# A hybrid decoder block: the down products in another order with four sums in one set of banks, gate operands one branch later, and four up weights in tiles of another pool

## The chip, the cores and the metric

The kernel runs on one core of a Trainium2 chip. The time is that of one execution on the device in microseconds; three timed runs of the kernel before gave 1117.07, 1119.05 and 1122.3 us, a median of 1119.05. One more execution was recorded by the hardware profiler: 1114.22 us, of which its span, from the first to the last recorded instruction, is 1112.4 us. Engines are called PE (the tensor engine; PEld is its weight load), DVE (vector), ACT (scalar), POOL (GpSimd) and SP, which here only issues transfers.

## The reference

One block on x of 1 x 1024 x 1024 in float32, with D_FF of 4096, cut to its core:

```
h = rmsnorm(x) @ w_in + b_in                 # 512 pool, 512 q, 128 k, 128 v, 2048 gates
y_pool = multiscale_pool(u) @ w_pool * pool_scale
y_attn = sliding window attention (window 128, 8 heads, 2 kv heads, sinks)
g_pool, g_attn = sigmoid(gates)
merged = g_pool * (y_pool @ w_branch_pool) + g_attn * (y_attn @ w_branch_attn)
x = x + rmsnorm(merged @ w_out)
ff = square(relu(rmsnorm(x) @ w_up)) @ w_down
return x + rmsnorm(ff)
```

## The kernel before

Every large product is made from pairs of reduced-precision operands: a value is split into a high half (a cast on ACT, line 101) and a low half (a subtraction on DVE, line 104), and PE runs three passes (high x high, low x high, high x low; PASSES). The largest products (gates, w_out, w_up, w_down) are cut into 2 x 2 blocks and computed with seven block products instead of eight, of which DVE forms sums and differences as operands and as results. So DVE and ACT prepare operands all the time and PE multiplies. Each engine works through its own queue in order; a scheduler of the tile framework sets those orders from the source and from priorities, so SP's order in particular is not that of the lines. Tiles come from pools of a fixed number of buffers; a load into a new tile waits for the last reader of the buffer's old tile.

Three places matter here.

**Gates (lines 913 to 1000).** The two branches are computed in eight steps m each. Step m makes one 128-row strip of a branch product in two "mm" banks (line 428), and DVE multiplies it into the gate tile z (line 933). Each step of even m loads two z tiles for two strips (line 922, "z loads", from the spilled gates). After each odd m, merge(m // 2) adds the pool branch's tiles to the attention branch's by two accumulating transfers on POOL (line 954, g<-g), for the last pair by DVE. From the merged tiles come the operands of the w_out products: gop[1] and gop[5] are made in steps m = 5 and 6 (lines 988 to 994) by split_pairs (high half, low half) and a subtraction (line 992). wo_weight loads the W_O weights of one product (line 970).

**Up products (lines 1200 to 1310).** The normalised x is transposed on PE (line 1081) from hs, which out_post makes for each of eight token tiles (lines 1039 to 1053): a load of x, mean square on ACT, reciprocal square root in small steps on DVE and ACT (lines 130 to 144), gain (line 1050), residual add (1051), store (1052). Pairs of w_up strips (UpPairs, 16 pairs; the first NF0 = 7 have their products 1 and 2 made early) are loaded (line 458) into a stage tile, and operand(p, i) splits them. prepare(p) is load(2p), operand(p, 1), operand(p, 2). The pool fp (12 tiles with tag "T") is opened here and is used for the third products' operands from build_second on.

**Down products (lines 1329 to 1476).** Seven products run in the order PRODUCTS, each over NS = 8 steps of two 128-row slices of D_FF, 192 matmuls a product, with operands made AHEAD = 2 steps before. Token tiles 0 to 3 (th = 0) and 4 to 7, and two column halves, make the four result blocks. A product sums over all its steps in four PSUM banks, "at" or "mm" in turn; 2 goes on top of 1 in the same banks, 3 on top of 5; the other sums are made by DVE from the copies u, v, c11, c12. The results get their square sums on ACT (fin_sq, line 1390), the gain on DVE (fin_gain, line 1393), rr by rsqrt_sum, and fin_out multiplies by rr, adds the x1 tile read from DRAM, and stores. The last product's last three steps (LATE) run token tile by token tile, so that each can be closed while PE works on the next.

Of the kernel before, what the change touches and what calls it, by code (L numbers as in the profile page):

```python
# [8 lines left out]
F32 = mybir.dt.float32  # L9
# [5 lines left out]
P = 128  # L15
# [3 lines left out]
NK = D // P  # L19
# [31 lines left out]
def block_kernel(ctx: ExitStack, tc, xt, x, consts, vecs, sinks, b_qkv, g_post, g_mlp_post,  # L51
# [20 lines left out]
    def stage(shape):  # L72
        return st.tile([P] + shape, F32, tag="st", name=nm("st"))
# [13 lines left out]
    def bank(tag, shape=None):  # L87
        return psum["pool"].tile([P] + (shape or [512]), F32, tag=tag, name=nm(tag), bufs=psum["bufs"][tag])
# [4 lines left out]
    def flat(t):  # L93
        return t.rearrange("p a b -> p (a b)")
# [879 lines left out]
    def merged(kh, th):  # L974
        return [zg[8, 2 * kh + j][th] for j in range(2)]

    def x_place(shape):
        return xp.tile([P] + shape, F32R, tag="x", name=nm("wo"))

    for m in range(8):  # L980
        branch(wbp_dram[m], lambda k, hl, th: ysp[k][hl][:, th * 512:(th + 1) * 512], 0, m)
        if m % 2:
            merge(m // 2)
        if m == 0:
            wo_weight(1, x_place)
        elif m == 2:
            wo_weight(5, x_place)
        elif m == 5:
            b11, b12 = merged(0, 1), merged(0, 0)
            gop[1] = split_pairs(b11, gr)  # L990
            for p_, q_ in zip(b11, b12):
                dve.tensor_tensor(p_, p_, q_, ALU.subtract)
        elif m == 6:
            gop[5] = split_pairs(b11, ar)
    xpool.__exit__(None, None, None)


# [234 lines left out]
        h, dj = B_OF[name]  # L1232
        return w_rows[s_, h][:, :, dj * 512:(dj + 1) * 512]

    up.prepare(3)
    up.prepare(4)
    up.load(0)
    up.load(1)
    def first_kt(kt):
# [8 lines left out]
    up.m2(0)  # L1248
    up.m2(1)
    up.m1(4, bank("mm"))  # L1250
    up.prepare(5)
    build_second(1)
    up.operand(0, 6)
    up.m1(5, bank("mm"))
    up.m2(2)
    up.prepare(6)
    build_second(2)
    build_third(0)
    up.operand(0, 7)
    up.m2(4)  # L1260
    up.m1(6, bank("mm"))
    b6, b7 = bank("at"), bank("at")
# [81 lines left out]
    def operands(i, s_):  # L1344

        if i == 1 and s_ in early_raw:
            ft, wt = early_raw[s_]
        else:
            ft = raw_tile()
            nc.sync.dma_start(ft, f_block(A_OF[i], s_))  # L1350
            if i == 1:
                resident("B11", s_)
                if s_ - 3 in early_raw:
                    resident("B11", s_ - 3)
                wt = res["B11", s_]
            elif i == 5:
                resident("B12", s_)
                wt = res["B11", s_]
                dve.tensor_tensor(wt, res["B12", s_], wt, ALU.subtract)  # L1359
            elif i == 2:  # L1360
                wt = streamed("B21", s_)
            elif i == 3:
                resident("B22", s_)
                wt = res["B22", s_]
            elif i == 6:
                wt = res["B11", s_]
                dve.tensor_tensor(wt, res["B22", s_], wt, ALU.subtract)
# [27 lines left out]
    def fin_half(n, dj, v):  # L1395
        fin_sq(n, dj, v)
        fin_gain(dj, v, v)
# [7 lines left out]
        dve.tensor_tensor(sq[:, dj, ns], sq[:, dj, ns], eps_y[:, ns], ALU.add)  # L1405

    def fin_out(n, hv):
        if n not in xf:
            t = stage([2, 512])
            nc.sync.dma_start(flat(t), x1_dram[n])  # L1410
            xf[n] = t
        for dj in (1, 0):
            o = xf[n][:, dj, :]
            dve.scalar_tensor_tensor(o, hv[dj][n % 4], rr[:, n:n + 1], o, ALU.mult, ALU.add)
            (nc.scalar if dj and n == NT - 1 else nc.sync).dma_start(out[n][:, dj * 512:(dj + 1) * 512], o)

    PRODUCTS = (1, 5, 2, 3, 6, 7, 4)
    LATE = 3
    steps = [(i, s_) for i in PRODUCTS for s_ in range(NS)]
    u, v, c11, c12 = acc4("u"), acc4("v"), acc4("c11"), acc4("c12")  # L1420
# [4 lines left out]
    for j, (i, s_) in enumerate(steps):  # L1425
        if j + AHEAD < len(steps):
            operands(*steps[j + AHEAD])
        if s_ == 0 and i not in (2, 3):
            tag = "mm" if i in (5, 7) else "at"
            banks[i] = [bank(tag) for _ in range(4)]  # L1430
        bs = banks[{2: 1, 3: 5}.get(i, i)]
        if i != 4 or s_ < NS - LATE:
            down_mm(i, s_, bs, i in (2, 3), [(s_, k2, t) for k2 in range(2) for t in range(4)])
            if s_ < NS - 1:
                continue
        elif s_ < NS - 1:
            continue
        for t in range(4):
            if i == 1:
                act.copy(u[t], bs[t])  # L1440
            elif i == 5:
                act.copy(v[t], bs[t])
            elif i == 2:
                act.copy(c11[t], bs[t])
                fin_half(t, 0, c11[t])
            elif i == 3:
                act.copy(c12[t], bs[t])
            elif i == 6:
                dve.tensor_tensor(u[t], u[t], bs[t], ALU.add)
                dve.tensor_tensor(c12[t], c12[t], u[t], ALU.add)  # L1450
                dve.tensor_tensor(v[t], v[t], u[t], ALU.add)
                fin_half(t, 1, c12[t])
            elif i == 7:
                dve.tensor_tensor(v[t], v[t], bs[t], ALU.add)
                dve.tensor_tensor(u[t], u[t], bs[t], ALU.add)
                fin_half(4 + t, 1, v[t])
            else:
                n = 4 + t
                down_mm(i, s_, bs, False, [(s2, k2, t) for s2 in range(NS - LATE, NS) for k2 in range(2)])
                dve.tensor_tensor(u[t], u[t], bs[t], ALU.add)  # L1460
                fin_sq(n, 0, u[t])
                fin_gain(0, c11[t], u[t])
                rsqrt_sum(rr[:, n:n + 1], sq[:, 0, n:n + 1], sq[:, 1, n:n + 1])
                fin_out(n, (c11, v))
        if i == 7:
            add_eps(slice(4, NT), 1)
            for n in range(4, NT):
                load_x1(n)
        if i == 6:
            add_eps(slice(0, 4), 1)  # L1470
            rsqrt_sum(rr[:, 0:4], sq[:, 0, 0:4], sq[:, 1, 0:4], 4)
            for n in range(4):
                fin_out(n, (c11, c12))
    rpool.__exit__(None, None, None)


# [70 lines left out]
```

## Time and profile before

| | before |
|---|---|
| timed runs | 1117.07, 1119.05, 1122.3 us; median 1119.05 |
| profiled execution | 1114.22 us |
| its span | 1112.4 us |
| mean granted clock | 1.00 in the windows shown below |
| DMA read, written | 152.99 MB, 63.96 MB |

A row of a timeline reads: start in us, length in us, engine, line, operation, out<-in, shape and count; in brackets how long the engine was idle just before and whom it waited for. A group row of a view by lines has the busy time of all, and the mean ns of one. SPq and POOLq rows are the issuing of transfers, not the transfers; "DMA" rows in the chain are the transfers. The names in out<-in are tile tags: g and gr, ar are gate tiles and operands, wh weight operands, st stage tiles, at and mm PSUM banks, sm small tiles of one column.

### The profile page before, as it was taken

The page shows a single profiled execution, that of the slowest core. Times are in us where ns is not written, and L with a number is a line of the kernel's source. Part 1 is how long each engine was busy: PE and PEld are TensorE (multiplying, and loading weights), DVE is VectorE, ACT ScalarE, POOL GpSimd, SP SyncE. Part 2 cuts the span into 40 slices and gives each one's busy share as a digit, 9 for nine tenths or more (in the row PEclk, how much of TensorE's full clock was granted, in tenths as well). Part 3 has the DMA queues.
Part 4 walks back from the last instruction along what each step waited for, and adds up shares of the span by engine and source line. Part 5 has one row for each costly group of instructions (what it writes and reads, how often), then busy time and mean ns, then how long its engine had stood idle before and what let it go on. Part 6 is the DMA issues. An engine that isn't in the chain of part 4 may idle for free.

```text
span 1112.4 us, 13921 instructions
## 1 busy us (share of the span) xinstructions
PE 1099.5 (99%) x5119; PEld 908.9 (82%) x5119; DVE 807.9 (73%) x1180; ACT 552.4 (50%) x921; POOL 59.8 (5%) x111
## 2 busy tenths in 40 slices
PE   9999999999999999999999999999999999999997
PEld 7888788888888878878888888888888888888885
DVE  5578867898868667989988767666548945447796
ACT  7466656444432326677555655444434435444342
POOL 0333221110000010000000000000000000000000
PEclk9999999999999999999999999999999999999999
DMA  9306569997676572563457645435697666332762
GB/s 349 140 11 136 149 147 344 232 318 248 216 250 221 152 186 74 195 232 109 145 202 259 243 174 195 155 143 209 216 363 247 231 192 196 104 96 73 223 191 81
DMA packets 91588, 212.63 MB, mean 191 GB/s; under 512 B 7616, under 2 KB 20032, under 8 KB 91456
## 3 DMA queue, kind: packets, MB, share of 16 engines
q1 hardware_dynamic: 78384, 180.54, 48.2%
q0 software_dynamic: 7520, 11.54, 6.3%
q10 hardware_dynamic: 5616, 19.66, 4.6%
q8 instruction: 40, 0.66, 0.2%
q14 instruction: 28, 0.23, 0.1%
HBM read 152.99 MB, written 63.96 MB: 195 GB/s over the span
## 4 chain that ended last, share of the span: by engine, by line
PE 82%; DVE 8%; DMA 5%; ACT 2%; issue 2%; DVEq 0%; POOL 0%; POOLq 0%; ACTq 0%; SPq 0%
PE mm L494 24%; PE at L494 16%; PE at L1384 15%; PE mm L1384 12%; PE mm L187 3%; PE mm L584 2%; PE at L1035 2%; DMA g<-g 1%; PE at L196 1%; PE mm L1035 1%; PE sc L187 1%; PE mm L428 1%; PE at L399 1%; DMA g<-spill_dram 1%; DVE gr L104 1%
## 5 line engine op out<-in xcount | busy, mean ns | idle before, releaser
L1384 PE MATMUL at<-ar,wh 128*128 128x512 f32 x744 | 169.6, 389 | 0.0
L1384 PEld LDWEIGHTS at<-ar,wh 128*128 128x128 f32 x744 | 139.6, 188 | 29.3 <-DVE ar L104 0.4
L1384 PE MATMUL mm<-ar,wh 128*128 128x512 f32 x576 | 131.0, 389 | 0.0
L104 DVE TENSOR_TENSOR wh<-raw,wh 128x1024 fp32r<-128x1024 f32 x53 | 64.8, 1223 | 89.7 <-ACT wh L101 89.7
L1384 PEld LDWEIGHTS mm<-ar,wh 128*128 128x128 f32 x576 | 108.1, 188 | 22.5
L101 ACT CAST wh<-raw 128x1024 fp32r<-128x1024 f32 x53 | 55.8, 1053 | 139.4 <-PE at L1384 62.4
L101 ACT CAST wh<-st 128x512 fp32r<-128x512 f32 (+1 forms) x107 | 68.4, 650 | 76.1 <-PE at L494 19.1
L104 DVE TENSOR_TENSOR wh<-st,wh 128x512 fp32r<-128x512 f32 (+1 forms) x107 | 76.8, 727 | 27.3 <-ACT wh L101 25.2
L494 PE MATMUL mm<-gr,wh 128*128 128x512 f32 x333 | 80.2, 391 | 0.0
L494 PEld LDWEIGHTS mm<-gr,wh 128*128 128x128 f32 x333 | 62.1, 188 | 12.8
L494 PE MATMUL mm<-T,wx 128*128 128x512 f32 x288 | 67.6, 389 | 0.0
L494 PEld LDWEIGHTS mm<-T,wx 128*128 128x128 f32 x288 | 54.1, 188 | 11.2
L494 PE MATMUL at<-T,wx 128*128 128x512 f32 x252 | 59.1, 389 | 0.0
L494 PEld LDWEIGHTS at<-T,wx 128*128 128x128 f32 x252 | 47.3, 188 | 9.8
L494 PE MATMUL mm<-x,wh 128*128 128x512 f32 x240 | 55.2, 389 | 0.0
L494 PEld LDWEIGHTS mm<-x,wh 128*128 128x128 f32 x240 | 45.0, 188 | 9.4
L584 PE MATMUL mm<-x,wh 128*128 128x512 f32 x192 | 47.8, 396 | 0.0
L104 DVE TENSOR_TENSOR ar<-B,ar 128x1024 fp32r<-128x1024 f32 x37 | 45.1, 1219 | 1.6 <-ACT ar L101 1.3
L584 PEld LDWEIGHTS mm<-x,wh 128*128 128x128 f32 x192 | 35.2, 188 | 7.7
L101 ACT CAST ar<-B 128x1024 fp32r<-128x1024 f32 x37 | 38.9, 1050 | 3.6 <-DVE B L1359 2.8
L494 PE MATMUL at<-gr,wh 128*128 128x512 f32 x150 | 36.6, 390 | 0.0
L101 ACT CAST wx<-ws 128x512 fp32r<-128x512 f32 x30 | 18.6, 620 | 33.9 <-DVE ws L470 19.1
(384 smaller groups left out, 2151.6 us busy)
## 6 DMA issues: line engine op xcount, KB each, us to landing
raw<-f_dram SPq DMA_DIRECT2D x53, 512.0 KB, 3.8
f_dram<-g SPq DMA_DIRECT2D x30, 512.0 KB, 3.3
st<-in_w_up_dram SPq DMA_DIRECT2D x24, 512.0 KB, 3.8
B<-in_w_dn_dram SPq DMA_DIRECT2D x24, 512.0 KB, 6.4
st<-in_w_g_dram SPq DMA_DIRECT2D x18, 512.0 KB, 6.9
f_dram<-g ACTq DMA_DIRECT2D x17, 512.0 KB, 3.0
g<-spill_dram SPq DMA_DIRECT2D x16, 512.0 KB, 6.3
raw<-in_w_dn_dram SPq DMA_DIRECT2D x16, 512.0 KB, 4.7
```

What stands on the lines that cost most here:

```text
L101: act.copy(hi, src)
L104: eng.tensor_tensor(lo, src, f32(hi), ALU.subtract)
L187: pe.matmul(bq, xs_[k][n // 4][:, xh, n % 4 * P:(n % 4 + 1) * P], wq[k][:, h, :], start=k == 0 and j == 0, stop=k == NK - 1 and j == 2)
L196: pe.matmul(bkv_of(n), xs_[k][n // 4][:, xh, n % 4 * P:(n % 4 + 1) * P], wkv[k // 2][:, h, k % 2, :], start=k == 0 and j == 0 and not (joi ...
L399: pe.matmul(flat(yb), v[:, kv, :], flat(p[:, 4 * kv:4 * kv + 4]), start=j == 0, stop=j == len(mms) - 1)
L428: pe.matmul(bs[th], whi[:, k, :], rhs(k, hl, th), start=k == 0 and hl == 0, stop=False)
L494: pe.matmul(b, w[:, wh, kt, :], xo[kt][:, xh, :], start=not after and kt == 0 and j == 0, stop=kt == 3 and j == 2, skip_group_check=after)
L584: pe.matmul(b, (whi, wlo)[h][:, k, :], xr(k, xh, th), start=j == 0, stop=j == len(mms) - 1)
L1035: pe.matmul(bs[t], gop[i][kt // 2][gh][:, kt % 2, t * P:(t + 1) * P], wop[i][kt // 2][wh][:, kt % 2], start=not after and kt == 0 and j == ...
L1384: pe.matmul(bs[t], fo[fh][:, k2, t * P:(t + 1) * P], wo_[wh][:, k2, :], start=not after and s2 == 0 and k2 == 0 and j == 0, stop=s2 == NS ...
```

## The change

It has three parts.

1. *Down order.* The order of products becomes 1, 5, 6, 3, 7, 2, 4. Products 1, 6, 7 and 4 sum in the same four "at" banks, 5 and 3 in "mm", and 2 in four "mm" banks of its own. The partial sums are read as they stand after a product: u after 1, v after 5, c12 after 6, v plus the bank after 7, and so on, so that twenty DVE additions go. The output of token tiles 0 to 3 is written in another way: x1 is copied to out from DRAM to DRAM by SP, ACT multiplies the results by rr in the steps s < 4 of product 4, and POOL adds them into out by accumulating transfers of 256 KB. For tiles 4 to 7 the square and the gain of the last product's results read its bank directly.
2. *Gate operands.* The operands gop[1] and the subtraction are made in m = 4 and 6 for one tile each, and gop[5] after the loop.
3. *Up weights.* The first strip of pairs 3 to 6 is loaded into a "T" tile of the pool fp (named wr), ahead of the first operands; prepare is gone there, and operand(0, 7) comes earlier.

```diff
+    b11, b12 = merged(0, 1), merged(0, 0)
     for m in range(8):
         branch(wbp_dram[m], lambda k, hl, th: ysp[k][hl][:, th * 512:(th + 1) * 512], 0, m)
...
-        elif m == 5:
-            b11, b12 = merged(0, 1), merged(0, 0)
-            gop[1] = split_pairs(b11, gr)
-            for p_, q_ in zip(b11, b12):
-                dve.tensor_tensor(p_, p_, q_, ALU.subtract)
-        elif m == 6:
-            gop[5] = split_pairs(b11, ar)
+        elif m in (4, 6):
+            j = m // 2 - 2
+            gop.setdefault(1, []).extend(split_pairs(b11[j:j + 1], gr))
+            dve.tensor_tensor(b11[j], b11[j], b12[j], ALU.subtract)
+    gop[5] = split_pairs(b11, ar)
...
-    up.prepare(3)
-    up.prepare(4)
+    for p in range(3, NF0):
+        up.load(2 * p, fp.tile([P, NK, P], F32, tag="T", name=nm("wr")))
+    for p in (3, 4):
+        for i in (1, 2):
+            up.operand(p, i)
...
             elif i == 3:
-                resident("B22", s_)
                 wt = res["B22", s_]
             elif i == 6:
+                resident("B22", s_)
                 wt = res["B11", s_]
...
-    PRODUCTS = (1, 5, 2, 3, 6, 7, 4)
+    PRODUCTS = (1, 5, 6, 3, 7, 2, 4)
...
-        if s_ == 0 and i not in (2, 3):
-            tag = "mm" if i in (5, 7) else "at"
-            banks[i] = [bank(tag) for _ in range(4)]
-        bs = banks[{2: 1, 3: 5}.get(i, i)]
+        if s_ == 0 and i in (1, 5, 2):
+            banks[i] = [bank("at" if i == 1 else "mm") for _ in range(4)]
+        bs = banks[{6: 1, 7: 1, 4: 1, 3: 5}.get(i, i)]
+        chained = i in (6, 7, 4, 3)
+        if i == 4 and s_ == 0:
+            add_eps(slice(0, 4), 1)
+            rsqrt_sum(rr[:, 0:4], sq[:, 0, 0:4], sq[:, 1, 0:4], 4)
+        if i == 4 and s_ < 4:
+            fin_gain(0, u[s_], u[s_])
+            for dj, t_ in ((1, c12[s_]), (0, u[s_])):
+                act.activation(t_, t_, AF.Identity, scale=rr[:, s_:s_ + 1])
+                pool.dma_start(out[s_][:, dj * 512:(dj + 1) * 512], t_, accum_op=ALU.add)
...
-            elif i == 2:
-                act.copy(c11[t], bs[t])
-                fin_half(t, 0, c11[t])
+            elif i == 6:
+                act.copy(c12[t], bs[t])
             elif i == 3:
-                act.copy(c12[t], bs[t])
-            elif i == 6:
-                dve.tensor_tensor(u[t], u[t], bs[t], ALU.add)
-                dve.tensor_tensor(c12[t], c12[t], u[t], ALU.add)
-                dve.tensor_tensor(v[t], v[t], u[t], ALU.add)
+                dve.tensor_tensor(c12[t], c12[t], bs[t], ALU.add)
                 fin_half(t, 1, c12[t])
             elif i == 7:
                 dve.tensor_tensor(v[t], v[t], bs[t], ALU.add)
+                fin_half(4 + t, 1, v[t])
+            elif i == 2:
                 dve.tensor_tensor(u[t], u[t], bs[t], ALU.add)
-                fin_half(4 + t, 1, v[t])
+                fin_sq(t, 0, u[t])
             else:
                 n = 4 + t
-                down_mm(i, s_, bs, False, [(s2, k2, t) for s2 in range(NS - LATE, NS) for k2 in range(2)])
-                dve.tensor_tensor(u[t], u[t], bs[t], ALU.add)
-                fin_sq(n, 0, u[t])
-                fin_gain(0, c11[t], u[t])
+                down_mm(i, s_, bs, True, [(s2, k2, t) for s2 in range(NS - LATE, NS) for k2 in range(2)])
+                fin_sq(n, 0, bs[t])
+                fin_gain(0, c11[t], bs[t])
                 rsqrt_sum(rr[:, n:n + 1], sq[:, 0, n:n + 1], sq[:, 1, n:n + 1])
...
         if i == 7:
             add_eps(slice(4, NT), 1)
             for n in range(4, NT):
                 load_x1(n)
-        if i == 6:
-            add_eps(slice(0, 4), 1)
-            rsqrt_sum(rr[:, 0:4], sq[:, 0, 0:4], sq[:, 1, 0:4], 4)
-            for n in range(4):
-                fin_out(n, (c11, c12))
+                nc.sync.dma_start(out[n - 4], x1_dram[n - 4])
```

How the change moves instructions shows on three queues. On SP, in the steps m of the pool branch, the kernel before has (st<-wbp_dram is a branch weight, st<-ws_dram a half of a W_O weight, g<-spill_dram a z load):

```order
L418 DMA st_3811<-wbp_dram 128x512
L970 DMA st_3932<-ws_dram 128x2x512
L970 DMA st_3934<-ws_dram 128x2x512
L922 DMA g_3765<-spill_dram 128x2x512
L922 DMA g_3766<-spill_dram 128x2x512
L970 DMA st_4000<-ws_dram 128x2x512
L970 DMA st_4002<-ws_dram 128x2x512
```

and the change, at the same place:

```order
L418 DMA st_3803<-wbp_dram 128x512
L922 DMA g_3760<-spill_dram 128x2x512
L922 DMA g_3761<-spill_dram 128x2x512
L970 DMA st_3932<-ws_dram 128x2x512
L970 DMA st_3934<-ws_dram 128x2x512
L970 DMA st_4000<-ws_dram 128x2x512
L970 DMA st_4002<-ws_dram 128x2x512
```

The two z loads have passed the two W_O loads, and the four of these now stand together. The orders of DVE, ACT and PE around them are the same in both.

On SP again, in the output products and the first up products, the kernel before has (x_dram<-st the store of the residual tile, st<-in_x_dram its load, st<-in_w_up_dram an up weight):

```order
L1052 DMA x_dram<-st_4225 128x1024
L1046 DMA st_4333<-in_x_dram 128x1024
L1052 DMA x_dram<-st_4261 128x1024
L1052 DMA x_dram<-st_4297 128x1024
L1046 DMA st_4385<-in_x_dram 128x1024
L1046 DMA st_4433<-in_x_dram 128x1024
L1052 DMA x_dram<-st_4333 128x1024
L1052 DMA x_dram<-st_4385 128x1024
L1046 DMA st_4491<-in_x_dram 128x1024
L1046 DMA st_4569<-in_x_dram 128x1024
L1052 DMA x_dram<-st_4433 128x1024
L458 DMA st_4596<-in_w_up_dram 128x1024
```

and the change:

```order
L1051 DMA x_dram<-st_4225 128x1024
L458 DMA wr_4596<-in_w_up_dram 128x1024
L458 DMA wr_4598<-in_w_up_dram 128x1024
L1051 DMA x_dram<-st_4261 128x1024
L1045 DMA st_4333<-in_x_dram 128x1024
L1051 DMA x_dram<-st_4297 128x1024
L1045 DMA st_4385<-in_x_dram 128x1024
L458 DMA wr_4600<-in_w_up_dram 128x1024
```

The weight of pair 3 (4596) has moved ahead of the residual's loads, into a tile of its own kind, and those of pairs 4 and 5 with it.

On DVE, at the end of the program, where the last token tile is closed, the kernel before has (u the sum, c the result with its gain, bc the gain, sm small tiles; in brackets the semaphores that are waited for):

```order
L1460 TENSOR_TENSOR u_7070<-u_7070,at_8952 128x512 [waits PE_49]
L1393 TENSOR_TENSOR c_1137_7078<-u_7070,bc_7052 128x512 [waits DVE_49]
L131 TENSOR_TENSOR sm_9265<-fsq 128x1 [waits Activation_49]
L136 RECIPROCAL sm_9268<-sm_9264 128x1 [waits Activation_49]
L139 SCALAR_TENSOR_TENSOR sm_9270<-sm_9268,sm_9265 128x1 [waits DVE_49]
```

and the change:

```order
L1397 TENSOR_TENSOR c_1137_7078<-at_7102,bc_7052 128x512 [waits Activation_49]
L131 TENSOR_TENSOR sm_9237<-fsq 128x1
L136 RECIPROCAL sm_9240<-sm_9236 128x1 [waits Activation_49]
L139 SCALAR_TENSOR_TENSOR sm_9242<-sm_9240,sm_9237 128x1 [waits DVE_49]
L143 TENSOR_SCALAR sm_9242<-sm_9242 128x1 [waits DVE_49]
```

The addition is gone, and the gain, which waited for DVE's own addition, now waits for ACT, whose square reads the same bank.

More of the change, by code (lines that the diff above doesn't have):

```diff
@@ L1250, in block_kernel @@
     up.m1(4, bank("mm"))
-    up.prepare(5)
+    up.operand(5, 1)
+    up.operand(5, 2)
     build_second(1)
@@ L1255, in block_kernel @@
     up.m2(2)
-    up.prepare(6)
+    up.operand(6, 1)
+    up.operand(6, 2)
+    up.operand(0, 7)
     build_second(2)
     build_third(0)
-    up.operand(0, 7)
     up.m2(4)
@@ L1407, in fin_out @@
     def fin_out(n, hv):
[L1408 to L1411, printed above, removed]
         for dj in (1, 0):
@@ L1427, in block_kernel @@
             operands(*steps[j + AHEAD])
-        if s_ == 0 and i not in (2, 3):
-            tag = "mm" if i in (5, 7) else "at"
-            banks[i] = [bank(tag) for _ in range(4)]
-        bs = banks[{2: 1, 3: 5}.get(i, i)]
+        if s_ == 0 and i in (1, 5, 2):
[10 more added lines that the diff above has]
+                pool.dma_start(out[s_][:, dj * 512:(dj + 1) * 512], t_, accum_op=ALU.add)
         if i != 4 or s_ < NS - LATE:
-            down_mm(i, s_, bs, i in (2, 3), [(s_, k2, t) for k2 in range(2) for t in range(4)])
+            down_mm(i, s_, bs, chained, [(s_, k2, t) for k2 in range(2) for t in range(4)])
             if s_ < NS - 1:
```

## The prediction

> **What bounds the kernel now.** The page's first part, its chain by engine, and the list of what TensorE (PE) waited for (what <- whom: us in total, times, longest):
>
> ```profile
> span 1112.4 us, 13921 instructions
> PE 1099.5 (99%) x5119; PEld 908.9 (82%) x5119; DVE 807.9 (73%) x1180; ACT 552.4 (50%) x921; POOL 59.8 (5%) x111
> PE 82%; DVE 8%; DMA 5%; ACT 2%; issue 2%; DVEq 0%; POOL 0%; POOLq 0%; ACTq 0%; SPq 0%
> PE at L1081 <- DVE x L1050: 1.6, 1, 1.6
> PE mm L205 <- DVE zeros L183: 1.5, 1, 1.5
> PE mm L428 <- DVE g L933: 1.0, 1, 1.0
> PE at L399 <- DVE qt L104: 0.4, 1, 0.4
> PE sc L335 <- DVE s L344: 0.3, 1, 0.3
> ```
>
> PE is busy for 1099.5 of 1112.4 us, and both kernels issue the same 5119 matmuls of the same shapes. So the vector and scalar work that the change removes is worth only the waits that it ends: all five named waits come to 4.8 us, and two of them, 1.6 and 1.0, lie where the change works. The down products are read next, in windows of one product each, the second and the last of seven (us, then PE, PEld, DVE, ACT, POOL busy with counts, granted clock, DMA share, GB/s):
>
> ```profile
> 843.10:886.60 43.50, 43.50 (x194) 36.02 (x193) 40.24 (x36) 18.19 (x21) 0.00 (x0) 1.00 0.71 235
> 1060.70:1104.50 43.80, 43.80 (x193) 35.62 (x191) 37.09 (x56) 17.81 (x29) 0.00 (x0) 1.00 0.40 132
> ```
>
> PE fills them, 43.50 busy of 43.50 at clock 1.00. DVE has 40.24 and 37.09 us there, and is not what PE waits for. Twenty DVE instructions taken from this phase give PE nothing. The program's end can gain only after the last matmul.
>
> **The change part by part.** The sum is made against the profiled execution's 1114.22 us, which is 4.83 below the 1119.05 median.
>
> **Down order and tail.** The tail of before, from the timeline:
>
> ```profile
> 1104.63 0.68 DVE L1460 TENSOR_TENSOR u<-u,at 128x512 f32<-128x512 f32 x1
> 1105.35 0.63 ACT L1390 ACTIVATE junk<-u 128x512 f32<-128x512 f32 x1 [2.92 <-DVE u L1460]
> 1105.35 0.69 DVE L1393 TENSOR_TENSOR c<-u,bc 128x512 f32<-128x512 f32 x1
> 1106.43 0.17 DVE L136 RECIPROCAL sm<-sm 128x1 f32<-128x1 f32 x1 [0.17 <-ACT sm L130]
> L1019 ACT ACTIVATE junk_o<-at 128x512 f32<-128x512 f32 x4 | 2.4, 588 | 0.0
> ```
>
> The add at 1104.63 goes; square and gain both read the bank. The square can start 1105.35 − 1104.63 = 0.72 us earlier, and from a bank it takes 0.59 (last row) for 0.63. But in the new program the gain waits for the square, where the two ran side by side at 1105.35. It then starts near 1105.35 again, behind the square's 0.59 and the read of its sum, and ends near 1106.05; the reciprocal behind it on DVE comes at about 1106.1 for 1106.43. **Gain 0.3**, bounds 0 (the square's root on ACT comes no earlier than the gain's end) and 0.7 (the gain does not hold the chain up). The Trainium skill, page "PSUM — Partial Sum Buffer", section "PSUM bank collisions raise a hardware error", says that two engines may not touch the same bank in the same partitions at once, two readers included, and that a dependency is put between them; it speaks against the full 0.72, and the order's wait agrees, though no run so far shows two readers of one bank.
>
> What the down order adds is eight ACT scales, eight accumulating POOL transfers of 256 KB and four DRAM copies. Nearest rows:
>
> ```profile
> g<-g POOLq DMA_DIRECT2D x6, 512.0 KB, 6.4
> L1091 ACT ACTIVATE raw<-at,vec 128x512 f32<-128x512 f32 x4 | 2.8, 688 | 1.1 <-DVE gr L1074 1.1
> ```
>
> 8 x 0.69 = 5.5 us of ACT in the last product, where ACT is busy for 17.81 of 43.80. The transfers are issued in its first four steps, 43.5 / 8 = 5.4 us each; the last starts near 1060.7 + 4 x 5.4 = 1082 and lands by about 1090 even if it needs the 6.4 us of twice its size. The end is at 1112, so they cost 0; only if all eight ran in single file from 1068 at 6.4 each (51 us, ending at 1119) would they cost 7. In the program each waits for its own copy, scale and semaphore, not for the others. The copies stand in the up phase and are needed 550 us later. That product's operands still come from DVE: four gains of 0.69 join it, the adds of before leave. **Cost 0**, bounds ±0.3 (one late operand).
>
> **Up weights of pairs 3 to 6.** The wait of 1.6, from the timeline:
>
> ```profile
> 464.30 0.33 SPq L1052 DMA_DIRECT2D x_dram<-st  x1
> 489.25 0.33 SPq L458 DMA_DIRECT2D st<-in_w_up_dram  x1
> 491.39 0.28 ACT L130 ACTIVATE sm<-sq,sm 128x1 f32<-128x1 f32 x1
> 492.16 0.15 DVE L143 TENSOR_SCALAR sm<-sm 128x1 f32<-128x1 f32 x1
> 492.99 0.62 ACT L101 CAST wh<-st 128x512 fp32r<-128x512 f32 x1 [1.31 <-DMA st<-in_w_up_dram]
> 493.64 0.69 DVE L104 TENSOR_TENSOR wh<-st,wh 128x512 fp32r<-128x512 f32 x1 [1.33 <-ACT wh L101]
> 494.25 0.15 DVE L144 TENSOR_TENSOR rr<-sm,sm 128x1 f32<-128x1 f32 x1
> 495.11 0.75 DVE L1050 SCALAR_TENSOR_TENSOR x<-at,rr,bc 128x512 f32<-128x512 f32 x1
> 495.91 0.66 PE L1081 MATMUL at<-cst,x 128*128 128x128 f32 x4 [1.59 <-DVE x L1050]
> ```
>
> Read upward: PE's transposes want x; x wants rr; rr stands on DVE behind the low half of pair 3's weight, which waits 1.33 for a cast, which waits 1.31 for a load issued only at 489.25, when its stage tile came free. In the change that weight goes to a tile of another pool, last read by an output product long before, and its load stands on SP right behind the store of 464.30. The cast can run as soon as ACT is free of the root at 491.39 + 0.28, so the low half starts at about 491.67 + 0.65 = 492.32 for 493.64, and everything behind it moves by 1.3. **Gain 1.3**; the rest of the wait, 0.3, is DVE's own chain. Bounds: 1.6 (all of it) and a loss of 1. The loss: DVE's queue in the pairs behind is reshuffled by one low half (0.69), and DVE has no slack there:
>
> ```profile
> 514.00:528.00 14.00, 14.00 (x72) 11.77 (x71) 13.90 (x23) 9.87 (x18) 0.00 (x0) 1.00 0.24 80
> 503.70 0.69 DVE L104 TENSOR_TENSOR wh<-st,wh 128x512 fp32r<-128x512 f32 x1 [1.26 <-ACT wh L101]
> ```
>
> 13.90 of 14.00. In its favour, a second wait of DVE (1.26 at 503.70, again a late w_up load) goes as well and hands DVE about as much as a reshuffle takes. What is pushed back on SP is the reads of x for the residual, by two loads of 0.33 issue and their time on the engines; two or three us of spare are an estimate from the store of 464.30 and the residual adds behind it, and I count 0.
>
> **Gate operands.** The wait of 1.0, from the chain in order of time (start, length, engine, what), then SP and two windows with the columns of above:
>
> ```profile
> 377.39 7.20 DMA g<-g
> 384.62 1.06 ACT gr L101
> 388.11 0.69 DVE g L933
> 389.96 9.38 DMA g<-g
> 399.37 1.06 ACT gr L101
> 402.94 0.61 DVE g L933
> 403.68 1.23 PE mm L428 x4
> 382.67 8.25 SPq L970 DMA_DIRECT2D st<-ws_dram  x2
> 390.97 4.31 SPq L922 DMA_DIRECT2D g<-spill_dram  x2
> 378.00:382.00 4.00, 4.00 (x19) 3.30 (x19) 1.25 (x3) 0.62 (x1) 0.45 (x1) 1.00 1.04 220
> 390.60:394.00 3.40, 3.40 (x17) 2.81 (x16) 2.92 (x4) 0.62 (x1) 0.51 (x1) 1.00 1.08 154
> 391.66 0.39 PE L428 MATMUL mm<-yphi,wh 128*128 128x512 f32 x1
> ```
>
> Two accumulating transfers g<-g, merge 0 (7.20 us) and merge 1 (9.38 us), head the chain. PE resumes 403.68 − 399.34 = 4.34 us after merge 1 lands, 1.0 later than it could. The order of DVE and ACT is the same in the change; what moves is on SP. The two z loads (g<-spill_dram, 1 MB) leave merge 1's time, where they were issued at 390.97 to 395.3, and stand ahead of the two W_O loads, and wait there only for a bank long read and for merge 0's first half, so they can issue from some 378 to 382, beside merge 0.
>
> Bounds. Say merge 0 takes d longer. The least is 0; the most by rows is 9.38 − 7.20 = 2.2, what the transfer took that had such loads beside it. DVE's multiply of 388.11, queued behind the operand that waits for merge 0, and merge 1 behind it, move by d. PE needs that multiply's bank at 391.66 and it is done at 388.80 (+0.6 for the other half): 2.2 us of spare, so nothing is lost there. Merge 1 then takes between 7.20 (freed of the loads) and 9.38 (it still has a W_O load of 390.9 beside it). PE's end moves by d + (its length − 9.38), not below −1.0, where the wait is gone: from −1.0 to +2.2. The row it is nearest to is the sum: two transfers that change places in 7.20 + 9.38 = 16.58 end at the same time. **Value 0.**
>
> The two windows price d in two ways. In 378 to 382 both queues moved data, 220 GB/s together; shared like this, merge 0 would lose one or two us. In 390.6 to 394 the engines were as full, but moved only 154 GB/s with the loads issued; if accumulating packets crowd the loads out like this, d is near 0. The value stands in between. The Trainium skill, "DMA: Bandwidth & Descriptors", section "Queues, rings and completion order", says that a DMA engine takes turns between its queues, packet by packet; by it d would be the first window's, and the sum 1 to 2 higher. The trace agrees in the first window and not plainly in the second.
>
> **Sum.** 1114.22 − 0.3 − 1.3 + 0 = 1112.6; plus the 4.83 to the median: **1117.4 us**.
>
> **Rivals.** (1) *Slower: the z loads delay merge 0 and merge 1 gets nothing back.* One place, PE at 403; it outweighs the gains of 1.6 once merge 1 lands more than 1.6 later. At d = 2.2 the time is 1119.05 − 1.6 + 2.2 = 1119.6; with twice that, 4.4, 1121.9. For it: engines at a share of 1.04 beside merge 0. Against it: the W_O loads no longer pass before. (2) *Merge 1, freed of 1 MB, lands early and the wait of 1.0 goes*: 1117.4 − 1.0 = 1116.4. For it: 154 GB/s while they met. Against: W_O still meets it. (3) *DVE's reshuffle*: DVE at 13.90 of 14.00 hands 0.69 to PE in three of the pairs, 2.1: 1119.5. (4) *The transfers of the tail run in single file, or the moves do nothing*: 1119 to 1124. Against it: the transfers wait on separate semaphores, and the moves are plain in the order of SP.
>
> **How the numbers follow.** Chances: forecast 0.5 (its own range 1116.5 to 1118.2); rival 1 0.25; rival 2 0.12; rival 3 0.08; rival 4 0.05. The range, 8 in 10, reaches by the cases from 1116.4 to 1119.6. The median itself is uncertain: the runs of before lie 2.0 below to 3.3 above theirs, and the profiled execution 4.83 below it. So 3.4 are added below and 1.9 above: 1113.0 to 1121.5. A measurement of this kernel can tell about 0.5% from no change, 5.6 us, which is more than all five waits together (4.8). So faster by over 0.5% 0.06, within 0.5% 0.88, slower 0.06.
>
> **What would show it.** Right: PE's wait for x at the transposes at 0.3 or less, PE's windows in the down products still full, the gain behind the square after the last matmul, reciprocal about 1.6 us after the last matmul's end (1104.50, the end of the last window) for 1.9. Wrong: a new wait of PE at the branches above 1.0 with a longer first g<-g; waits of PE for DVE in 500 to 600; an accumulating transfer landing after 1104; or a fall by more than 5 us, which would mean that PE's own pace, not its waits, had changed.

## The result, and the profile after

Over 22 runs each, the changed kernel takes 1122.09 us (1117.74 to 1128.46) and the kernel before 1116.52 (1112.73 to 1125.71): ratio 1.0047, interval 1.0029 to 1.0066. So it is slower by about 5.2 us, where 1.6 faster was forecast. (The forecast of 1117.4 stands on the first three runs of before, whose median of 1119.05 lies 2.5 above that of the 22; set against 1117.4 alone, the miss would look smaller than it is.) The profiled execution of the change took 1119.47 us, 5.25 more than that of before.

The page's first part and the list of what PE waited for, after:

```profile
span 1117.7 us, 13904 instructions
PE 1101.4 (99%) x5119; PEld 910.3 (81%) x5119; DVE 794.3 (71%) x1160; ACT 555.3 (50%) x925; POOL 66.7 (6%) x119
PE mm L428 <- DVE g L933: 3.6, 1, 3.6
PE at L1388 <- ACT ar L101: 2.0, 1, 2.0
PE mm L205 <- DVE zeros L183: 1.5, 1, 1.5
PE mm L494 <- DVE z L522: 0.9, 1, 0.9
PE at L1080 <- DVE x L1049: 0.5, 1, 0.5
```

DVE has 13.6 us less to do, and PE waits more. The wait at the branches (L428) went from 1.0 to 3.6, the one at the transposes from 1.6 to 0.5, and two are new: 2.0 in the down products, and 0.9 at L494 near 260 us, where both kernels issue the same instructions in the same order. That last one comes and goes between executions (0 to 3.8 us in the kernels below), so it is not put down to the change.

**Branches.** The chain in order of time, after:

```profile
378.50 9.24 DMA g<-g
...
393.11 9.93 DMA g<-g
403.06 1.06 ACT gr L101
404.14 1.24 DVE gr L104
405.40 1.23 DVE g L992
406.62 0.61 DVE g L933
407.37 1.23 PE mm L428 x4
```

Merge 0 takes 9.24 where it took 7.20, and merge 1 takes 9.93 where it took 9.38: +2.04 and +0.55, together the 2.6 by which PE's wait grew. SP's timeline shows the z loads beside merge 0 and the W_O loads behind them; the four of the second row are issued at 384.54, 393.69, 396.62 and 410.13, so that two of them lie beside merge 1:

```profile
378.70 5.67 SPq L922 DMA_DIRECT2D g<-spill_dram  x2
384.54 25.95 SPq L970 DMA_DIRECT2D st<-ws_dram  x4
```

**Last step of product 4.** The chain of after, then windows: the first of after, up to the wait, the second the same 26 us of the kernel before, the third after again, behind the wait:

```profile
1082.98 9.85 DMA raw<-in_w_dn_dram
1092.86 1.24 DVE raw L1377
1094.11 1.05 ACT ar L101
1095.21 15.48 PE at L1388 x60
```

```profile
1066.70:1092.80 26.10, 26.10 (x116) 21.59 (x116) 17.13 (x22) 14.95 (x21) 7.04 (x8) 1.00 0.94 238
```

```profile
1064.40:1090.50 26.10, 26.10 (x117) 21.61 (x116) 22.11 (x23) 11.53 (x14) 0.00 (x0) 1.00 0.50 161
```

```profile
1095.20:1096.50 1.30, 1.29 (x3) 0.86 (x4) 1.22 (x2) 0.00 (x0) 0.00 (x0) 0.50 0.00 0
```

The last weight load of the program takes 9.85 us; the page's median for these sixteen loads is 4.7. POOL's accumulating transfers run beside it: two are under way when it is issued, three more are issued by 1089.42, and the last lands at 1095.05. The DMA engines are at 0.94 where they were at 0.50. By the packets in the two traces, SP's loads have 0.50 of the engines' time in both windows, and POOL's queue has another 0.44 in the change and nothing in before. The sum made from that load (L1377), the cast and the low half behind it are late, and PE starts again at 1095.21, 2.40 after its last matmul's start, where 0.23 is usual: 2.2 are lost, of which the list of waits has 2.0. Then the granted clock is 0.50: matmuls take 427 ns from start to start instead of 227 until 1098.4, which costs 1.7 us more.

**Tail**, after (PE's last matmul ends at 1110.67):

```profile
1110.71 0.60 ACT L1394 ACTIVATE junk<-at 128x512 f32<-128x512 f32 x1 [3.06 <-PE at L1388]
1111.43 0.69 DVE L1397 TENSOR_TENSOR c<-at,bc 128x512 f32<-128x512 f32 x1 [1.16 <-ACT junk L1394]
1112.11 0.15 DVE L136 RECIPROCAL sm<-sm 128x1 f32<-128x1 f32 x1
```

The gain does stand behind the square. The reciprocal comes 1.44 us behind the last matmul (1.93 before), and the span ends 7.02 behind it (7.95 before).

In this pair of executions: +2.6 and -1.1 of waits, +2.2 and +1.7 (clock) in product 4, +1.1 near 260, -0.9 in the tail, some 0.3 less in small gaps: +5.3.

### The profile page after: what moved, and what is told of

It reads as the page before. It is cut to its first block, busy times and chain, and to the rows that moved or that the text cites. A ratio compares the mean times of both kernels' runs of the same rounds, so it can differ in the third digit from the quotient of the medians.

```text
span 1117.7 us, 13904 instructions
## 1 busy us (share of the span) xinstructions
PE 1101.4 (99%) x5119; PEld 910.3 (81%) x5119; DVE 794.3 (71%) x1160; ACT 555.3 (50%) x925; POOL 66.7 (6%) x119
## 4 chain that ended last, share of the span: by engine, by line
PE 82%; DVE 8%; DMA 5%; ACT 2%; issue 2%; DVEq 0%; POOL 0%; SPq 0%; POOLq 0%; ACTq 0%
PE mm L494 22%; PE at L494 15%; PE at L1388 14%; PE mm L1388 12%; PE mm L428 4%; PE mm L187 3%; PE mm L584 2%; PE at L1034 2%; PE mm L430 2%; DMA g<-g 2%; PE at L196 1%; PE mm L1034 1%; DMA g<-in_w_g_dram 1%; PE sc L187 1%; DMA raw<-in_w_dn_dram 1%
## 5 line engine op out<-in xcount | busy, mean ns | idle before, releaser
L1388 PE MATMUL mm<-ar,wh 128*128 128x512 f32 x576 | 131.0, 389 | 0.0
L101 ACT CAST wh<-st 128x512 fp32r<-128x512 f32 (+1 forms) x99 | 63.1, 653 | 72.6 <-PE at L494 14.1
L104 DVE TENSOR_TENSOR wh<-st,wh 128x512 fp32r<-128x512 f32 (+1 forms) x99 | 71.1, 729 | 24.3 <-ACT wh L101 22.3
L494 PE MATMUL mm<-gr,wh 128*128 128x512 f32 x333 | 80.3, 391 | 0.0
L494 PEld LDWEIGHTS mm<-gr,wh 128*128 128x128 f32 x333 | 62.1, 188 | 13.0 <-DVE gr L1073 0.3
L494 PE MATMUL mm<-T,wx 128*128 128x512 f32 x288 | 67.6, 389 | 0.0
L494 PEld LDWEIGHTS mm<-T,wx 128*128 128x128 f32 x288 | 54.1, 188 | 11.2
L494 PE MATMUL at<-T,wx 128*128 128x512 f32 x252 | 59.2, 389 | 0.0
L494 PE MATMUL mm<-x,wh 128*128 128x512 f32 x240 | 55.3, 389 | 0.1
L494 PEld LDWEIGHTS at<-T,wx 128*128 128x128 f32 x252 | 47.3, 188 | 9.8
L494 PEld LDWEIGHTS mm<-x,wh 128*128 128x128 f32 x240 | 45.0, 188 | 9.7 <-issue 0.5
L1439 POOL DMA_DIRECT2D out_dram<-c x4 | 4.0, 998 | 667.8 <-ACT c L1438 664.1
L494 PE MATMUL at<-gr,wh 128*128 128x512 f32 x150 | 36.6, 390 | 0.0
```

Source lines behind the costliest of these rows:

```text
L101: act.copy(hi, src)
L104: eng.tensor_tensor(lo, src, f32(hi), ALU.subtract)
L494: pe.matmul(b, w[:, wh, kt, :], xo[kt][:, xh, :], start=not after and kt == 0 and j == 0, stop=kt == 3 and j == 2, skip_group_check=after)
L1388: pe.matmul(bs[t], fo[fh][:, k2, t * P:(t + 1) * P], wo_[wh][:, k2, :], start=not after and s2 == 0 and k2 == 0 and j == 0, stop=s2 == NS ...
L1439: pool.dma_start(out[s_][:, dj * 512:(dj + 1) * 512], t_, accum_op=ALU.add)
```

## The experiments

All are timed beside the kernel before on the same chip, and the ratios are to it.

**The parts one at a time.** Each is the kernel before with the diff lines of one part, or of two.

> The kernel before with part 2 (gate operands) alone. Theory T, the z loads lie beside merge 0 and lengthen it, and merge 1 gets nothing back: merge 0 takes about 9.2 us instead of 7.2, PE waits 3.6 at the branches instead of 1.0, +2.6 us, ratio 1.0023. Rival E, it was that one execution: wait near 1.0, ratio 1.000.

Measured: 1.0037 (1.0017 to 1.0056). Merge 0 took 9.25, merge 1 9.96, and PE waited 3.6. Windows of this kernel, the wait and what follows it:

```profile
405.90:409.70 3.80, 0.21 (x1) 0.01 (x1) 3.17 (x4) 1.25 (x2) 0.00 (x0) 1.00 0.00 2
409.70:413.90 4.20, 4.18 (x12) 3.14 (x13) 2.75 (x3) 2.26 (x3) 1.79 (x2) 0.62 0.60 109
```

Theory T stands, E falls. Here the wait has the slow clock behind it (0.62 over 4.2 us), which it had not in the changed kernel's execution.

> The kernel before with part 3 (up weights) alone. Theory T: the wait for x at the transposes falls from 1.6 to 0.5, -1.1 us, ratio 0.9990, and nothing is lost in the pairs behind. Rival, the reshuffled DVE order costs PE 0.7 at some places in 500 to 600: waits there, ratio 1.000 or more.

Measured: 1.0009 (0.9989 to 1.0030). The wait is 0.5, as T has it, and the pairs behind have none; but no gain can be measured (T's 0.9990 lies at the edge of the interval).

> The kernel before with part 1 (down order and the accumulating output) alone. Theory T, the accumulating transfers crowd the last operand loads of the last product: PE waits about 2 us for the operand of the last step of product 4, runs some 3 us behind it at half the granted clock (1.7 us more), and the tail behind the last matmul is 0.9 shorter: +3.0 us, ratio 1.0027. The waits of 1.0 at the branches and of 1.6 at the transposes stay as they were. Rival E, the wait in the changed kernel's profile was of that one execution: no such wait, and -0.9 us.

Measured: 1.0123 (1.0094 to 1.0152), and neither theory. The wait at the last step is there (1.5, behind a load of 9.38 us), but most of the loss lies in the up phase, which this part was not thought to touch. From PE's waits:

```profile
PE mm L494 <- DVE wh L104: 3.1, 2, 2.9
PE at L1081 <- ACT x L1053: 1.7, 1, 1.7
PE mm L494 <- ACT wh L101: 1.2, 1, 1.2
```

The orders of PE, DVE and ACT differ there from those of before: SP has the four copies x1 to out between the residual's stores and the up weights, and the scheduler has put the weights' halves later. The same stretch of up products takes 11.2 us more than in before.

> Parts 1 and 3 without part 2 (gate operands undone). Theory T: the wait at the branches is back at 1.0, the up phase has no waits beyond 0.5 (part 3's early loads hide what part 1's copies did to it alone), the wait of about 2 us at the last step of product 4 stays, and the tail is 0.9 shorter: -1.1 - 0.9 + 2.2, with up to 1.7 more where a slow clock follows the wait: ratio 1.000 to 1.002. Rival, part 1's trouble in the up phase is not hidden by part 3 alone: waits there, ratio over 1.005.

Measured: 1.0021 (0.9999 to 1.0043). The wait at the branches is 0.9, that at the transposes 0.3, the up phase is clean: with part 3 ahead of them the copies do no harm. The wait at the last step is 3.3, behind a load of 11.09 us. Theory T.

> Part 1 alone, with the output of token tiles 0 to 3 by load, DVE and SP's stores, so without the four copies that stood in the up phase, and without accumulating. Theory C, the copies made the scheduler's other order in the up phase and the 10 us there: no waits between 497 and 560 beyond the 1.6 at the transposes, a wait of about 1.3 at the last step of product 4, tail 0.5 to 0.9 shorter: ratio 1.000 to 1.001. Rival: the longer waits of the up phase stay: ratio over 1.005.

The edit, on part 1 alone:

```diff
         if i == 4 and s_ < 4:
             fin_gain(0, u[s_], u[s_])
-            for dj, t_ in ((1, c12[s_]), (0, u[s_])):
-                act.activation(t_, t_, AF.Identity, scale=rr[:, s_:s_ + 1])
-                pool.dma_start(out[s_][:, dj * 512:(dj + 1) * 512], t_, accum_op=ALU.add)
+            fin_out(s_, (u, c12))
...
-                nc.sync.dma_start(out[n - 4], x1_dram[n - 4])
```

Measured: 0.9990 (0.9964 to 1.0017). The up phase is back in before's order, without the waits: theory C, though ACT's scales and POOL's transfers went together with the copies. (The kernel with plain stores, below, has the copies and no accumulating, and loses the same 11.2.) The wait at the last step is 0.2, less than expected. The wait at the transposes is 0.4 here, although nothing is changed at that place; more of that below.

**Branches: the z loads moved out of merge 0.**

> Part 2 alone, with the two z loads of the last pair issued two strips earlier, so that they are done before merge 0; the order of the operands is the change's. Theory T, the z loads beside merge 0 made the wait: merge 0 takes about 7.2, merge 1 less than 9.4, the wait at the branches is between 0 and 1.0, ratio 0.999 to 1.000. Rival O, the order of the operands made it: merge 0 near 9.2, or the wait at 3.6, ratio 1.0037 as part 2 alone.

```diff
         elif m in (4, 6):
+            if m == 4:
+                gate_pair(0, 3)
             j = m // 2 - 2
```

Measured: 0.9987 (0.9963 to 1.0010). The chain and the wait:

```profile
378.20 7.43 DMA g<-g
...
391.01 8.92 DMA g<-g
PE mm L428 <- DVE g L933: 0.8, 1, 0.8
```

The order of the operands is the change's, and the loss is gone: the z loads beside merge 0 made it, not the operands. Rival O falls.

**Last step: what crowds the load.**

> Part 1 alone, with POOL's eight transfers into out as plain stores without the accumulation, so that out of token tiles 0 to 3 lacks x1. ACT's eight scales, POOL's eight issues and the bytes written stay. Theory T, the accumulating packets crowd the loads: the wait at the last step falls to 0.5 or less and the time to 0.9 below before, ratio 0.9992. Rival A, ACT's scales (5.6 us) hold up the casts of the operands: the wait of about 2 us and the slow clock stay, ratio 1.0027. Rival Q, any transfer of POOL's queue does it: the same as A, but with the operand's load late.

```diff
-                pool.dma_start(out[s_][:, dj * 512:(dj + 1) * 512], t_, accum_op=ALU.add)
+                pool.dma_start(out[s_][:, dj * 512:(dj + 1) * 512], t_)
```

Measured: 1.0112 (1.0082 to 1.0143); the copies are still in, and so is the trouble of the up phase, which the expected ratio left out. In product 4, where the question lies, PE waits for nothing. The window of this kernel that ends where the operand was late in the others:

```profile
1080.00:1106.00 26.00, 26.00 (x116) 21.53 (x115) 19.90 (x25) 16.32 (x25) 4.40 (x8) 1.00 0.72 244
```

ACT's scales and POOL's eight issues are in it, at a DMA share of 0.72, not 0.94, for as many GB/s. By the packets, POOL's queue has 0.20 of the engines' time here for 2.1 MB, and had 0.44 in the change for 2.0 MB. So rival A falls, and rival Q as far as the wait goes: it is the accumulating that fills the engines. But plain stores lengthen the last load too. From its issue to the sum that wants it are 6.8 us here:

```profile
1098.03 0.37 SPq L1341 DMA_DIRECT2D raw<-in_w_dn_dram  x1
1104.88 1.22 DVE L1373 TENSOR_TENSOR raw<-raw,B 128x1024 f32<-128x1024 f32 x1
```

It was not late enough for PE to wait. The plain stores are also issued sooner, the last at 1095.07, before that load, where three of the accumulating ones stood behind it. This run does not separate the later issue from the time that each transfer takes of the engines; the last kernel below, with plain stores behind the load's issue, bears on it.

> Parts 1 and 3, with ACT's eight scales and POOL's accumulating transfers held until the last operand of product 4 is built. Theory T, the transfers crowd the operand loads: the wait at the last step falls to 0.5 or less, and the end does not come later, since the transfers land before the last stores: -2.0, ratio 0.998. Rival A (ACT's scales or DVE's gains make the operand late, not the transfers): these are moved too, so the wait falls as well; the plain stores told these two apart. Rival L, the transfers land after the last stores: the tail grows by some us, ratio 1.001 or more.

```diff
-        if i == 4 and s_ < 4:
+        if i == 4 and s_ == NS - LATE:
+            zl, rl = sp.tile([P, 4], ...), sp.tile([P, 4], ...)
+            lo = opers[4, NS - 1][1][1][:, 1, 508:512]
+            dve.tensor_tensor(zl, lo, lo, ALU.subtract)
+            dve.tensor_tensor(rl, rr[:, 0:4], zl, ALU.add)
...
-                act.activation(t_, t_, AF.Identity, scale=rr[:, s_:s_ + 1])
+                    act.activation(t_, t_, AF.Identity, scale=rl[:, n:n + 1])
```

Measured: 1.0084 (1.0060 to 1.0107). The wait is gone, but most matmuls from 225 us on are longer, which no theory had: in the down products their pitch, the time from one start to the next, is 228.9 ns for 226.7. So the time says nothing about L; the tail of 10.3 us, for 7.0 in the change, speaks for it. In place of two tiles of 16 bytes a partition, zl and rl were put into one of 512:

> Parts 1 and 3 with the accumulating transfers held until the last operand is built, as before, but with the two helper columns in one tile of 512 bytes, so that nothing behind it is shifted off. Theory P and L: the matmul pitch is 226.7, the wait at the last step is gone, and the tail is some 3 us longer than the changed kernel's since the transfers and the last stores share the engines: -1.1 and +2.3 against before, ratio 1.001.

Measured: 1.0011 (0.9990 to 1.0033), no wait at the last step, pitch as before. Behind the last matmul, this kernel and then the kernel before:

```profile
1103.68:1113.80 10.12, 0.00 (x0) 0.00 (x0) 3.98 (x10) 0.98 (x3) 0.88 (x1) 0.71 0.84 227
```

```profile
1104.50:1112.40 7.90, 0.00 (x0) 0.00 (x0) 3.78 (x10) 1.02 (x3) 0.00 (x0) 0.71 0.36 134
```

The tail is 3.1 longer than the changed kernel's: held back, the transfers share the engines with the last stores. T and L both hold; there is no free place for them at this end of the program.

> All three parts, with the z loads two strips earlier and the accumulating transfers held behind the last operand. Theory T: both new waits are gone, the one at the transposes stays at 0.5, the tail 0.9 shorter, and the one at the branches between 0 and 1.0: 2.0 to 3.0 below before, ratio 0.997 to 0.998. Rival: one of the waits was made by something else and stays.

Measured: 1.0084 (1.0058 to 1.0111). The wait at the branches is 0.8 and that at the last step gone, but it has the two small tiles as well, and the longer matmuls and the tail outweigh both.

**The longer matmuls.** The edit is one line in the kernel before, `sp.tile([P, 8], F32, tag="pd", ...)`, with 16 in the second.

> The kernel before with 32 bytes a partition allocated and left unused in the pool of small tiles, so that the tiles behind it lie 32 bytes on; no instruction changes. Theory P, the two new tiles of 16 bytes in the held-back kernels shifted the operands and made every matmul about 1 per cent longer (pitch 228.9 ns for 226.7): the same pitch here, +9 us or so, ratio 1.008. Rival: the pitch belongs to those executions or to something else in those kernels: 226.7 and 1.000.

> As the kernel with 32 bytes, with 64 bytes. Theory P with a grain of 64 bytes: pitch 226.7, ratio 1.000. With a coarser grain: 228.9 and 1.008.

Measured: 1.0143 (1.0096 to 1.0190, from two runs) with 32 bytes, 1.0050 (1.0028 to 1.0072) with 64. All engines' instructions stand in the same order. The same group of 576 down matmuls with 32 bytes, with 64, and in the kernel with the tile of 512:

```profile
L1386 PE MATMUL mm<-ar,wh 128*128 128x512 f32 x576 | 134.9, 395 | 0.0
```

```profile
L1386 PE MATMUL mm<-ar,wh 128*128 128x512 f32 x576 | 132.3, 391 | 0.0
```

```profile
L1389 PE MATMUL mm<-ar,wh 128*128 128x512 f32 x576 | 131.0, 389 | 0.0
```

By 576 that is 234, 230 and 227 ns a matmul; before has 131.0 too. P stands, with a grain above 64 bytes. The two kernels with the tiles of 16 bytes have the row of 64 bytes (132.3, 391) and not that of 32, although their tiles come to 32 bytes; why is open. The changed kernel, whose pitch is before's, is cleared.

**Without accumulating.**

> All three parts with the z loads two strips earlier, and the output of token tiles 0 to 3 written as in the kernel before (load of x1, multiply and add on DVE, stores by SP), at the place of the change, without the four copies and the accumulating transfers. Theory T: nothing accumulates into out, so the wait at the last step falls to 0.5 or less and the tail keeps its 0.9: transposes -1.1, tail -0.9, branches 0 to -0.2: ratio 0.998. Rival S, the stores stand on SP ahead of the last operand loads and wait for DVE, so that the operand is late again: a wait of 1 us or more there, ratio 1.000 or more.

The edit of the kernel without copies, on all parts with the early z loads. Measured: 0.9990 (0.9966 to 1.0013). Rival S, for the wait: the fourth x1 load waits on SP for a stage tile, the stores stand ahead of the weights, and the last operand is 1.1 late:

```profile
1074.51 5.61 DMA st<-x_dram
...
1082.03 5.56 DMA raw<-in_w_dn_dram
```

> Parts 2 and 3 with the z loads two strips earlier; the down products are those of the kernel before. Theory T: the waits at the branches (0.8 to 1.0) and at the transposes (0.5 or less) are what the two parts leave; nothing changes behind. 1.1 to 1.3 below before: ratio 0.999.

Measured: 0.9974 (0.9953 to 0.9995): the change without its down part, with the z loads early, is faster than before.

> All three parts with the z loads two strips earlier; token tiles 0 to 3 are closed by DVE (multiply and add of x1, loaded early into free tiles) and stored by POOL without accumulating, so that SP holds nothing but operand loads in the last product. Theory T: the wait at the last step is 0.5 or less, and all gains stand: -1.1 at the transposes, -0.2 at the branches, -0.9 in the tail: ratio 0.998. Rival: the down order itself leaves the last operands no time (DVE's gains and multiplies ahead of them): a wait of 1 us or more stays.

```diff
+        if i == 2 and s_ == 0:
+            for n in range(4):
...
+                    nc.sync.dma_start(flat(t), x1_dram[n])
...
             for dj, t_ in ((1, c12[s_]), (0, u[s_])):
-                act.activation(t_, t_, AF.Identity, scale=rr[:, s_:s_ + 1])
-                pool.dma_start(out[s_][:, dj * 512:(dj + 1) * 512], t_, accum_op=ALU.add)
+                o = x1h[s_][dj]
+                dve.scalar_tensor_tensor(o, t_, rr[:, s_:s_ + 1], o, ALU.mult, ALU.add)
+                pool.dma_start(out[s_][:, dj * 512:(dj + 1) * 512], o)
```

Measured: 0.9967 (0.9944 to 0.9989), 1114.15 against 1116.60: faster than both kernels. No wait in the down products, 0.7 at the branches, tail 7.07:

```profile
1066.00:1092.00 26.00, 26.00 (x115) 21.23 (x115) 23.56 (x31) 10.04 (x10) 4.38 (x8) 1.00 0.66 223
```

DVE has 6.4 us more there than in the change and is still not waited for. Two of POOL's plain stores are issued at 1082.35 and 1083.06, behind the last weight load (1081.36), and that load takes 5.0.

## Why the prediction was wrong, step by step

- **What bounds the kernel**: right. PE's waits are the account, and the DVE work removed gave nothing.
- **Gate operands, value 0**: this step failed. It took "two transfers that change places" for the row nearest: merge 0 was to lose what merge 1 gains. Merge 0 lost 2.04, near the bound of 2.2, and merge 1 gained nothing. In before four loads are issued beside it, two of z and two of W_O, and in the change the two of W_O alone; yet at 9.93 it lay above the bound of 9.38. With the same two and the z loads moved out of merge 0 it took 8.92, so without 1 MB of loads beside it merge 1 gains 0.5 at best; why it was 9.93 in the change is open. That is rival 1, given a chance of 0.25; +2.6 in both executions, and gone with the z loads moved. The first of the two windows, where both queues moved data, pointed that way; I set it against one with other loads in it. What the Trainium skill says ("DMA: Bandwidth & Descriptors", section "Queues, rings and completion order") gave a sum 1 to 2 higher, the better one by merge 0's 9.24.
- **Accumulating transfers, cost 0**: this step failed too. It asked when they land, and they did land in time. The last was issued at 1089.42 and landed at 1095.05, where the prediction had 1082 and 1090. It did not ask what was under way beside them: the last operand load, which had little to spare. In before:

```profile
1086.27 1.23 DVE L1373 TENSOR_TENSOR raw<-raw,B 128x1024 f32<-128x1024 f32 x1 [0.49 <-DMA raw<-in_w_dn_dram]
1088.72 1.05 ACT L101 CAST ar<-raw 128x1024 fp32r<-128x1024 f32 x1
```

The sum made from the load ends at 1087.50 and ACT takes it up at 1088.72, so the load could land some 1.2 us later and move nothing (an estimate from these two rows). In the change it took 9.85 us, where 4.7 lie between its issue in before (1081.57) and this sum, and PE waited 2.0, 1.5 and 3.3 in three kernels; plain stores made no wait.
- **Up weights, gain 1.3**: mechanism right as far as shown, the size wrong. The first two of the moved loads are issued from 468.77 on, where pair 3's was issued at 489.25, and the wait fell to 0.5. But 1.6 was that one execution's: in kernels that leave this place as it was, it is 1.6, 0.6, 0.8, 1.2, 0.4 and none (before, part 2 alone, early z loads, 64 bytes, part 1 without copies, 32 bytes), 0.8 on the mean. With part 3 it is 0.3 to 0.5 in six kernels and none in three, 0.3 on the mean. The term is about 0.5, and alone it did not show.
- **The four copies, cost 0**: true only beside part 3. With part 1 alone the scheduler's order changes and some 11 us are lost.
- **Tail, gain 0.3**: mechanism right, the size low: 0.5 at the reciprocal, and 0.4 more in the last store, which varies by as much between kernels. What the Trainium skill says ("PSUM — Partial Sum Buffer", section "PSUM bank collisions raise a hardware error") agrees: the gain starts at 1111.43, behind the square's read of its sum, and not beside it.
- **Not in the sum: the clock.** I priced a wait by its length. Behind waits of over 2 us the granted clock fell to half in several executions. Over the runs, the mean clock is 0.9946 for the change (22 runs) and 0.9971 for before (104 runs, those beside the experiments); as a share of 1117 us that is an estimate of 2.8 us, about half of the loss. The rest is the waits: 2.6 + 2.2 - 0.5 - 0.9 = 3.4 by the figures above. Together 6.2, within the 3.2 to 7.4 that the interval gives. The split is an estimate; no run held the clock. The means also take in each program's end, where no matmul runs and the clock falls too (0.71 in the last window of before shown above); that end is 0.9 shorter in the change, so the clock's part in the stages may be up to 0.5 more.

## What to carry to other kernels

A transfer that lands in time can still cost: look which load with little slack it shares the engines with, and keep accumulating transfers away from it. A wait read from one execution is a sample, so a term of one or two microseconds needs the same wait in several kernels that do not touch it. A part that looks harmless may be so only because another part of the change stands in front of it.

## What the runs showed of the hardware that was not expected

- **Half clock behind a wait.** Before PE's last matmul, the granted clock is at 0.50 in nine stretches in all these traces together. Seven are 3.41 us long and two 6.83, and stretches of one trace begin a whole number of 3.41 us apart (43 times in the kernel with part 2 alone, from 263.93 to 410.70). A wait of 2.0 in the change was followed by one and its wait of 3.6 was not. Periods of 3.41 us counted from the stretch at 1095.20 put the 2.0 into one period and split the 3.6 into 1.90 and 1.66. Counted so in every trace, all eight periods in which PE was idle for 2.0 us or more were followed by half clock, and those with up to 1.9 were not, but for three (1.8, 1.7 and 0.7) in the up phase of the two kernels with part 1 alone, one of them with plain stores. So the same wait can cost 1.7 more or nothing, by where it falls. This is read off the traces, and no run tried it. The Trainium skill, page "TensorE: Matmul & The Clock Gate", section "What's actually happening", gives a free-running window of about 3.4 us and a fall to half after an idle one. The length of the slow stretches and their places agree; that 2.0 us of idle time were enough does not, if the window must be idle throughout.
- **The pitch of a matmul depends on where its operands lie.** With 32 bytes a partition allocated ahead of them the down matmuls took 3 per cent longer (234 ns for 227), with 64 bytes 1 per cent (230), with 512 nothing, at a clock of 1.00 in the down products. Which operand does it was not tried.
- **Accumulating transfers keep the DMA engines busy.** In product 4, 238 GB/s took a share of 0.94 with them and 244 GB/s a share of 0.72 with plain stores. In merge 0 of the change, a packet of g<-g (4 KB) held its engine for 335 ns on the mean, and one of the loads beside it (2 KB) for 85.
